# Pinning the input-gate product behind the recurrence's decay, with a tile of its own for the decay

## The chip, the core and the metric

The kernel runs on one core of one Trainium2 chip. The metric is the device time of one execution in microseconds (us); less is better. A core has five engines that matter here, each working through its own queue of instructions in order: PE (matrix products; PEld is its weight load), DVE (elementwise work and scans), ACT (functions and casts), POOL (small elementwise work and some DMA issues) and SP (DMA issues). An instruction starts when it is first in its queue and the semaphores that it waits for have been raised by other engines or by landed DMAs.

## The reference, cut to what matters

A trunk of two post-norm layers over 512 tokens of width 1024, in float32. The first layer (even) projects the input into eight retention heads and eight blocks of a gated linear recurrence (RG-LRU), multiplies both branches by SiLU gates, and maps them back; the second (odd) is differential attention. The change concerns the recurrence alone:

```
def rg_lru_branch(xb, conv_w, conv_b, wa, ba, wx, bx, lam):
    xc = causal_depthwise_conv(xb, conv_w) + conv_b
    xg = xc.reshape(B, S, LRU_BLOCKS, LRU_BLOCK_DIM)
    r = jax.nn.sigmoid(jnp.einsum('bsgi,gij->bsgj', xg, wa).reshape(B, S, W) + ba)
    i = jax.nn.sigmoid(jnp.einsum('bsgi,gij->bsgj', xg, wx).reshape(B, S, W) + bx)
    log_a = -LRU_C * r * jax.nn.softplus(-lam.astype(jnp.float32))
    a = jnp.exp(log_a)
    u = xc * i * jnp.sqrt(-jnp.expm1(2.0 * log_a))
    _, h = lax.associative_scan(combine, (a, u), axis=1)   # h = a * h_before + u
    return h
```

## The kernel before, in words

Activations lie with features on the 128 partitions and the 512 tokens along the row, so that a projection block is one 128x512 bank of PSUM. Every float32 operand of a product is split into a high part (a cast, L153, on ACT) and a low part (a subtraction, L154, on DVE), and each product is three matmuls (L158): high by high, low by high, high by low. A name that ends in h or l is such a part: k3h and k3l are the parts of head 3's key, w33h and w33l those of weight block 33.

The even layer runs over eight heads and eight recurrence blocks. Its projections are listed in one order: gl and gr (the gates), xb (the recurrence's input), q and k, out (a piece of the output projection). The smaller steps of retention and recurrence are generators that a helper (Side.tick) advances between the projection's matmuls. PE and SP run in the order in which the program is traced (manual_schedule). DVE, ACT and POOL are ordered by a scheduler, which works with priorities (the P_ numbers) and its own estimate of durations; the order is fixed when the kernel is built. keep_in_program_order pins an instruction behind the one that was traced last on its engine.

One recurrence block (lru) goes: L555 and L557 copy and scale the projection's bank xb_ps on ACT, which frees that bank; three L561 on DVE make the convolved block xc, which L153 and L154 split; PE makes the gates' products pr and pi; ACT takes the sigmoids (L570 to t, L575 to i) and a tanh (L577). L578 on DVE multiplies i by xc, the product that the change is about. Then d, made on DVE by L584 and L585 with two ACT results, the logarithm L582 and the exponential L583 in r, is the recurrence's decay; it is written over xc. L586 is a square root on ACT, L587 to L589 make the recurrence's factors, L590 is the scan, L593 applies the gate gl, and the result is split for the output projection (lrum). The tile i is the tile xb, so that L578 is the last reader of xc and L589 the first reader of the product.

Retention, beside it, makes scores rs by blocks (L515 on DVE multiplies by the decay mask dec, freeing one of two banks that pr and pi share), splits them (r20 is head 2, block 0), sums them with v into ro, squares (L526) and splits that into rq, and sums rq's square over the head by a product with ones (rv, L532 and L533). L537 to L548 normalize the head and apply gr.

Temporaries of both come from one pool of ten 128x512 tiles (es); the gate weights gw, which SP loads, take their place in it too. Projection banks are four and go round. Weights are loaded through three buffers w_r, each reused when the low part of the block three before has been made.

Of the kernel before, what the change touches and what calls it, by code (L numbers as in the profile page):

```python
# [11 lines left out]
ALU = mybir.AluOpType  # L12
# [92 lines left out]
def trunk(ctx: ExitStack, tc: tile.TileContext, a):  # L105
    nc = tc.nc
# [25 lines left out]
    def temp(name):  # L132
        return es.tile([P, S], F32, tag="es", name=name)

    def bank(pl, tag, name):
        return pl.tile([P, 512], F32, tag=tag, name=name)
# [4 lines left out]
    def part(n, name):  # L141
        return pair(sp, [P, n], f"s{n}", name, bufs=full if n == S else 1)

    def cut(t, *ix):
        return t[0][ix], t[1][ix]

    def split(src, dst, scale=None, copy=nc.scalar.copy):
        if scale is not None:
            s = sg[:, scale:scale + 1]
            nc.scalar.activation(out=dst[0], in_=src, func=AF.Identity, scale=s)  # L150
            nc.vector.scalar_tensor_tensor(out=dst[1], in0=src, scalar=s, in1=dst[0].bitcast(F32), op0=ALU.mult, op1=ALU.subtract)
            return
        copy(out=dst[0], in_=src)  # L153
        return nc.vector.tensor_tensor(out=dst[1], in0=src, in1=dst[0].bitcast(F32), op=ALU.subtract)  # L154

    def mm3(out, l, r, start, stop, kinds=range(3), **kw):
        for n in kinds:
            nc.tensor.matmul(out=out, lhsT=l[n == 2], rhs=r[n == 1], start=start and n == 0, stop=stop and n == 2, **kw)  # L158
# [392 lines left out]
    def lru(c, ps, m):  # L551

        with tc.high_priority(P_OUT if c in OUT_NEXT else P_CONV):
            xb = temp(f"xbp{c}")
            nc.scalar.copy(out=xb, in_=ps)  # L555
            xc = temp(f"xc{c}")
            nc.scalar.activation(out=xc, in_=ps, func=AF.Identity, scale=conv_w(3, c), bias=conv_b(c))  # L557
        with tc.high_priority(P_CONV):
            for w in range(3):
                sh = 3 - w  # L560
                nc.vector.scalar_tensor_tensor(out=xc[:, sh:], in0=xb[:, :S - sh], scalar=conv_w(w, c), in1=xc[:, sh:], op0=ALU.mult, op1=ALU.add)  # L561
        with tc.high_priority(P_OUT if c in OUT_NEXT or c == 7 else P_GATES):
            t2 = part(S, f"xc{c}")
            split(xc, t2)
        yield LRU_GATES[c]
        pr = bank(ps_sc, "sc", f"pr{c}")
        o = c % 2 * 2 * P
        mm3(pr, cut(gw[0], ALL, slice(o, o + P)), t2, True, True)
        t = temp(f"t{c}")
        nc.scalar.activation(out=t, in_=pr, func=AF.Sigmoid, bias=gba(c))  # L570
        yield 1
        pi = bank(ps_sc, "sc", f"pi{c}")
        mm3(pi, cut(gw[0], ALL, slice(o + P, o + 2 * P)), t2, True, True)
        i = xb
        nc.scalar.activation(out=i, in_=pi, func=AF.Sigmoid, bias=gbx(c))  # L575

        nc.scalar.activation(out=t, in_=t, func=AF.Tanh, scale=sp4[:, c:c + 1])  # L577
        nc.vector.tensor_tensor(out=i, in0=i, in1=xc, op=ALU.mult)  # L578
        d = xc
        r = temp(f"r{c}")  # L580

        nc.scalar.activation(out=r, in_=t, func=AF.Ln, bias=1.0)  # L582
        nc.scalar.activation(out=r, in_=r, func=AF.Exp, scale=-1.0)  # L583
        nc.vector.scalar_tensor_tensor(out=d, in0=t, scalar=1.0, in1=r, op0=ALU.add, op1=ALU.mult)  # L584
        nc.vector.scalar_tensor_tensor(out=d, in0=d, scalar=2.0, in1=r, op0=ALU.subtract, op1=ALU.mult)  # L585
        nc.scalar.activation(out=r, in_=t, func=AF.Sqrt)  # L586
        nc.vector.scalar_tensor_tensor(out=t, in0=t, scalar=1.0, in1=d, op0=ALU.subtract, op1=ALU.mult)  # L587
        nc.vector.scalar_tensor_tensor(out=r, in0=r, scalar=-2.0, in1=d, op0=ALU.mult, op1=ALU.mult)
        nc.vector.tensor_tensor(out=r, in0=r, in1=i, op=ALU.mult)  # L589
        nc.vector.tensor_tensor_scan(out=d, data0=t, data1=r, initial=0.0, op0=ALU.mult, op1=ALU.add)  # L590
        if ("gl", c) not in gates:
            yield lambda: 0 if ("gl", c) in gates else math.inf
        nc.vector.tensor_tensor(out=d, in0=d, in1=gates.pop(("gl", c)), op=ALU.mult)  # L593
        split(d, cut(m, ALL, c % 2))
# [18 lines left out]
    for kind, i in ev:  # L613
        if kind == "v":
            if i:
                for j in range(4):
                    side.need(job["ret", j], lambda: j in seen)
            v = v_even(i)
        elif kind == "xb":
            if i % 2 == 0:  # L620
                raw = load(f"gw{i}", [P, 4 * P], a["gw"][i // 2], pl=es, tag="es")
                gw[0] = pair(two, [P, 4 * P], "gw", f"gw{i}", bufs=1)
                split(raw, gw[0])
            job["lru", i] = side.add(lru(i, t_unit(x, f"xb{i}"), mixes(("lru", i // 2))), "lru", 2)
        elif kind == "q":
            dec[i] = load(f"dec{i}", [P, S], a["dec"][i], pl=two, tag="dec")
            q[i] = rope(t_unit(x, f"q{i}"), "q", f"q{i}")
        elif kind == "k":
            job["ret", i] = side.add(retention(i, q.pop(i), rope(t_unit(x, f"k{i}"), "k", f"k{i}"), v, dec.pop(i), mixes(("ret", i // 2))), "ret", 1, RET_START[i])
        elif kind in ("ro", "lo", "out"):  # L630
            even_out({"ro": ("ret",), "lo": ("lru",), "out": ("lru", "ret")}[kind], i, f"{kind}{i}")
        else:
            ps = t_unit(x, f"{kind}{i}")
            if len(users) >= 5:
                side.need(job[users[-5]])
            users.append(("ret" if kind == "gr" else "lru", i))
            g = gp.tile([P, S], F32, tag="g", name=f"{kind}{i}")
            with tc.high_priority(P_OUT if kind == "gl" and i in OUT_NEXT else 0):
                silu(ps, g, f"{kind}{i}")
            gates[kind, i] = g  # L640
# [425 lines left out]
```

## Time and profile before

| what | value |
|---|---|
| median of 3 runs | 919.75 us (917.55 to 919.83) |
| the profiled execution | 919.09 us, its span 917.3 us (1.8 us lie around the span) |
| PE busy | 904.7 us, 99% of the span |
| DVE busy | 717.7 us, 78% |
| ACT busy | 518.1 us, 56% |
| mean granted TensorE clock | 0.997 |

PE's busy time is an overlap: a 128x512 matmul is shown as 0.39 us long, and the next one starts 0.23 us after it. Whether PE stood still is read from the distance between starts, and not from the busy time.

### The profile page before, as it was taken

What the parts mean: (1) busy time and instruction counts of PE and PEld (TensorE: products, weight loads), DVE (VectorE), ACT (ScalarE), POOL (GpSimd) and SP (SyncE); (2) the same over time, 40 slices, a digit from 0 to 9 for tenths busy, and PEclk for the clock granted to TensorE, in tenths of its full rate; (3) what the DMA queues carried; (4) which work ended last, traced back from release to release, by engine and by line L of the source; (5) the groups of instructions that cost most, each with busy time, mean ns of one, the idle gap of its engine ahead of it and who ended that gap; (6) DMA issues with size and microseconds to landing.
All of it is one profiled execution on the core that took longest, in us unless ns stands there. A gap on an engine that the chain in (4) does not pass through costs nothing.

```text
span 917.3 us, 11876 instructions
## 1 busy us (share of the span) xinstructions
PE 904.7 (99%) x4258; PEld 750.2 (82%) x4258; DVE 717.7 (78%) x1191; ACT 518.1 (56%) x847; POOL 111.5 (12%) x190
## 2 busy tenths in 40 slices
PE   8999999999999999999999999999999999999996
PEld 6888887888888888888888878888887888888885
DVE  5877977978868998897778787748867668877687
ACT  5567796656575668532455666435755355665440
POOL 2311010120102010010101110000110100201112
PEclk9999999999999999999999999999999999999998
DMA  8985463682829372434942126547247282186102
GB/s 287 290 273 149 129 182 91 190 258 58 267 78 279 100 210 78 154 113 155 335 164 79 62 68 237 222 165 249 70 138 271 119 319 93 60 284 255 45 1 92
DMA packets 46524, 152.93 MB, mean 167 GB/s; under 512 B 6145, under 2 KB 6273, under 8 KB 45697
## 3 DMA queue, kind: packets, MB, share of 16 engines
q1 hardware_dynamic: 41472, 135.39, 41.8%
q0 software_dynamic: 4992, 16.78, 9.4%
q8 instruction: 33, 0.54, 0.2%
q14 instruction: 27, 0.21, 0.1%
HBM read 139.57 MB, written 37.75 MB: 193 GB/s over the span
## 4 chain that ended last, share of the span: by engine, by line
PE 87%; DVE 5%; ACT 3%; issue 2%; POOL 1%; DMA 1%; SPq 0%; DVEq 0%; ACTq 0%; POOLq 0%
PE oo_ps L158 8%; PE q_ps L158 5%; PE gr_ps L158 5%; PE gl_ps L158 4%; PE k_ps L158 4%; PE xb_ps L158 4%; PE ev_ps L158 4%; PE out_ps L158 4%; PE po L158 3%; PE as L158 3%; PE ov_ps L158 2%; PE gv3a L158 2%; PE eo_ps L158 2%; PE og_ps L158 2%; PE gv2a L158 2%; PE gv3b L158 2%
## 5 line engine op out<-in xcount | busy, mean ns | idle before, releaser
L701 ACT ACTIVATE e<-as,nm 128x128 f32<-128x128 f32 (+3 forms) x64 | 33.2, 523 | 33.2 <-DVE nm L698 33.0
L708 POOL TENSOR_SCALAR zr<-z 128x1 f32<-128x1 f32 x32 | 16.3, 510 | 248.7 <-ACT e L701 248.7
L740 DVE SCALAR_TENSOR_TENSOR o<-po,ars,og 128x256 f32<-128x256 f32 x32 | 15.5, 484 | 35.9 <-POOL ars L396 35.9
L187 POOL DMA_DIRECT2D t<-t x24 | 18.9, 788 | 160.9 <-DMA t<-in_od_w 160.9
L187 POOL DMA_DIRECT2D t<-in_od_w x24 | 19.0, 793 | 117.6 <-DMA t<-in_od_w 117.5
L737 POOL TENSOR_SCALAR ave<-ss,zr 128x1 f32<-128x1 f32 x32 | 15.8, 493 | 142.0 <-ACT po L734 133.7
L698 DVE CUSTOM_DVE_ANT_0 as<-as,mask 128x128 f32<-128x128 f32 (+3 forms) x64 | 30.4, 505 | 2.3 <-PE as L158 2.3
L734 ACT ACTIVATE po<-po 128x256 f32<-128x256 f32 x32 | 11.9, 371 | 25.6 <-PE po L158 25.3
L396 POOL TENSOR_TENSOR ars<-ave,nhalf 128x1 f32<-128x1 f32 x32 | 18.8, 586 | 2.7
L578 DVE TENSOR_TENSOR xbp<-xbp,xc 128x512 f32<-128x512 f32 x8 | 5.5, 691 | 17.0 <-ACT xbp L575 17.0
L709 DVE SCALAR_TENSOR_TENSOR e<-e,zr,e 128x128 f32<-128x128 f32 (+3 forms) x32 | 17.6, 549 | 0.8
L561 DVE SCALAR_TENSOR_TENSOR xc<-xbp,vecs,xc 128x509 f32<-128x509 f32 (+2 forms) x24 | 17.8, 744 | 0.2
L396 POOL TENSOR_TENSOR lrs<-lve,nhalf 128x1 f32<-128x1 f32 x8 | 7.3, 911 | 82.1 <-DVE lve L410 82.1
L279 DVE TENSOR_TENSOR y<-oo_ps,y 128x512 f32<-128x512 f32 x23 | 15.3, 684 | 2.2 <-PE oo_ps L158 2.2
L515 DVE TENSOR_TENSOR rsd<-rs,dec 128x512 f32<-128x512 f32 (+3 forms) x32 | 15.3, 482 | 0.7 <-PE rs L158 0.5
L570 ACT ACTIVATE t<-pr,vecs 128x512 f32<-128x512 f32 x8 | 5.5, 687 | 17.3 <-PE pr L158 17.3
L713 PE MATMUL wt<-ident,e 128*128 128x128 f32 x80 | 13.9, 272 | 0.0
L153 ACT CAST hh<-ht 128x512 fp32r<-128x512 f32 x8 | 4.7, 588 | 15.4 <-PE ht L658 15.4
L713 PEld LDWEIGHTS wt<-ident,e 128*128 128x128 f32 x80 | 10.5, 140 | 3.4
L586 ACT ACT_TABLE_LOAD x8 | 10.3, 1283 | 4.2 <-DVE xc L585 4.1
L701 ACT ACTIVATION_READ_ACCUMULATOR e<-as,nm 128x1 f32 x64 | 12.5, 195 | 0.0
L744 PEld LDWEIGHTS po<-ident,o 128*128 128x128 f32 x64 | 8.9, 140 | 4.2
(2844 smaller groups left out, 3472.6 us busy)
## 6 DMA issues: line engine op xcount, KB each, us to landing
w_r<-in_od_w SPq DMA_DIRECT2D x58, 512.0 KB, 5.9
w_r<-in_ev_w SPq DMA_DIRECT2D x47, 512.0 KB, 5.6
t<-in_od_w SPq DMA_DIRECT2D x48, 256.0 KB, 5.7
sx<-sd SPq DMA_DIRECT2D x24, 512.0 KB, 6.2
w_r<-t SPq DMA_DIRECT2D x24, 512.0 KB, 3.2
w_r<-in_ev_wo SPq DMA_DIRECT2D x16, 512.0 KB, 4.2
w_r<-in_od_wo SPq DMA_DIRECT2D x16, 512.0 KB, 4.8
t<-in_od_w POOLq DMA_DIRECT2D x24, 256.0 KB, 5.7
```

The lines of the kernel that those rows point to most:

```text
L158: nc.tensor.matmul(out=out, lhsT=l[n == 2], rhs=r[n == 1], start=start and n == 0, stop=stop and n == 2, **kw)
L187: nc.gpsimd.dma_start(out=dst, in_=two, max_dma_last_dim=4 * D, accum_op=ALU.add)
L279: nc.vector.tensor_tensor(out=yy, in0=ps, in1=yy, op=ALU.add)
L396: nc.gpsimd.tensor_tensor(out=out, in0=var, in1=nhalf[:, :1], op=ALU.pow)
L561: nc.vector.scalar_tensor_tensor(out=xc[:, sh:], in0=xb[:, :S - sh], scalar=conv_w(w, c), in1=xc[:, sh:], op0=ALU.mult, op1=ALU.add)
L698: nc.vector.tensor_tensor_reduce(out=ps[:, :n], in0=ps[:, :n], in1=mask[:, S - n:], scale=-QK_SCALE, scalar=3.0e38, op0=ALU.add, op1=ALU.m ...
L701: nc.scalar.activation(out=e, in_=ps[:, :n], func=AF.Exp, scale=-1.0, bias=nm, accum_out=z[:, mp:mp + 1])
L708: nc.gpsimd.tensor_scalar(out=zr[:, 1:2], in0=z[:, 0:1], scalar1=z[:, 0:1], scalar2=EPS, op0=ALU.mult, op1=ALU.mult)
L709: nc.vector.scalar_tensor_tensor(out=ee[0], in0=ee[1], scalar=zr[:, 0:1], in1=ee[0], op0=ALU.mult, op1=ALU.add)
L713: nc.tensor.transpose(out=pt[:, kb * P:kb * P + P], in_=ee[0][:, kb * P:kb * P + P], identity=ident)
L737: nc.gpsimd.tensor_scalar(out=ve, in0=ss, scalar1=zr[:, 1:2], scalar2=None, op0=ALU.add)
L740: nc.vector.scalar_tensor_tensor(out=o, in0=po[:, :2 * P], scalar=rs, in1=gates[qb, hd // 2][:, hc:hc + 2 * P], op0=ALU.mult, op1=ALU.mult)
```

## The change

The decay d gets a tile of its own from the pool of temporaries, so xc stays whole while d is made. The product of i and xc is traced behind the two operations that make d, and is pinned behind the second of them. One more tile per block is taken from the pool of ten; the number of operations on DVE, PE, POOL and SP stays the same. L578 becomes L585, and L582 to L585 become L581 to L584.

```diff
@@ lru @@
         nc.scalar.activation(out=t, in_=t, func=AF.Tanh, scale=sp4[:, c:c + 1])
-        nc.vector.tensor_tensor(out=i, in0=i, in1=xc, op=ALU.mult)
-        d = xc
+        d = temp(f"d{c}")
         r = temp(f"r{c}")
 
         nc.scalar.activation(out=r, in_=t, func=AF.Ln, bias=1.0)
         nc.scalar.activation(out=r, in_=r, func=AF.Exp, scale=-1.0)
         nc.vector.scalar_tensor_tensor(out=d, in0=t, scalar=1.0, in1=r, op0=ALU.add, op1=ALU.mult)
         nc.vector.scalar_tensor_tensor(out=d, in0=d, scalar=2.0, in1=r, op0=ALU.subtract, op1=ALU.mult)
+        tc.keep_in_program_order(nc.vector.tensor_tensor(out=i, in0=i, in1=xc, op=ALU.mult))
         nc.scalar.activation(out=r, in_=t, func=AF.Sqrt)
```

The scheduler answers with another order on DVE and ACT through the whole even layer; PE, SP and POOL keep theirs. Three places follow, each as it stands in the program before and then in the changed one.

On ACT, where block 3's bank is read (the projection that follows it is a piece of the output, out), before:

```order
L153 CAST lrum1h<-xc_1063 128x512
L555 COPY xbp_1379<-xb_ps 128x512
L557 ACTIVATE xc_1381<-xb_ps,vecs 128x512
L153 CAST retm0h<-rq_1168 128x512
L153 CAST r20h<-rsd_1328 128x512
L153 CAST r21h<-rsd_1370 128x384
```

and now:

```order
L153 CAST lrum1h<-d_1204 128x512
L153 CAST r20h<-rsd_1331 128x512
L153 CAST retm0h<-rq_1170 128x512
L555 COPY xbp_1382<-xb_ps 128x512
L557 ACTIVATE xc_1384<-xb_ps,vecs 128x512
L153 CAST r21h<-rsd_1373 128x384
```

The two reads of the bank, L555 and L557, moved behind two casts, one of a score block and one of retention's result.

On DVE, in block 4's turn, where head 3's squares are split (rq3l), before:

```order
L154 TENSOR_TENSOR w36l<-w_r,w36h 128x1024
L154 TENSOR_TENSOR rq3l<-rq_1950,rq3h 128x512
L154 TENSOR_TENSOR q4l<-q_c,q4h 128x512
L584 SCALAR_TENSOR_TENSOR xc_1825<-t_1909,r_1921 128x512
L585 SCALAR_TENSOR_TENSOR xc_1825<-xc_1825,r_1921 128x512
```

and now:

```order
L154 TENSOR_TENSOR w36l<-w_r,w36h 128x1024
L154 TENSOR_TENSOR q4l<-q_c,q4h 128x512
L583 SCALAR_TENSOR_TENSOR d_1924<-t_1913,r_1925 128x512
L584 SCALAR_TENSOR_TENSOR d_1924<-d_1924,r_1925 128x512
L154 TENSOR_TENSOR rq3l<-rq_1955,rq3h 128x512
L585 TENSOR_TENSOR xbp_1827<-xbp_1827,xc_1829 128x512
```

rq3l moved from in front of q4l and the two steps of d to behind them, and the product stands behind it.

On DVE, in block 6's turn, from the key's last step to the split of head 5's third score block (r52l), before:

```order
L384 TENSOR_TENSOR k_c<-k_c,k_s 128x512
L154 TENSOR_TENSOR r53l<-rsd_2850,r53h 128x128
L584 SCALAR_TENSOR_TENSOR xc_2695<-t_2774,r_2786 128x512
L154 TENSOR_TENSOR k6l<-k_c,k6h 128x512
L585 SCALAR_TENSOR_TENSOR xc_2695<-xc_2695,r_2786 128x512
L154 TENSOR_TENSOR r52l<-rsd_2806,r52h 128x256
```

and now:

```order
L384 TENSOR_TENSOR k_c<-k_c,k_s 128x512
L584 SCALAR_TENSOR_TENSOR d_2791<-d_2791,r_2792 128x512
L585 TENSOR_TENSOR xbp_2699<-xbp_2699,xc_2701 128x512
L154 TENSOR_TENSOR k6l<-k_c,k6h 128x512
L515 TENSOR_TENSOR rsd_2813<-rs_2809,dec_2556 128x256
L515 TENSOR_TENSOR rsd_2857<-rs_2853,dec_2556 128x128
L279 TENSOR_TENSOR y<-lo_ps_2848,y 128x512
L154 TENSOR_TENSOR r53l<-rsd_2857,r53h 128x128
L587 SCALAR_TENSOR_TENSOR t_2780<-t_2780,d_2791 128x512
L588 SCALAR_TENSOR_TENSOR r_2792<-r_2792,d_2791 128x512
L154 TENSOR_TENSOR r52l<-rsd_2813,r52h 128x256
```

The product and the mask step of that block came from in front of the key's first step to behind its last one, and one y step (L279) and two steps of the recurrence (L587, L588) now stand ahead of r52l.

## Rows read from the trace of the kernel before

**Rows 1.** The page's first part, PE's row: busy us, share of the span and instructions, for PE and the other engines.

```profile
PE 904.7 (99%) x4258; PEld 750.2 (82%) x4258; DVE 717.7 (78%) x1191; ACT 518.1 (56%) x847; POOL 111.5 (12%) x190
```

**Rows 2.** The view of busy time by stretches, the even layer from 48 to 412 us: length, then busy us (and instructions) of PE, PEld, DVE, ACT and POOL, then the granted clock, the DMA engines' share and GB/s.

```profile
48.00:412.00 364.00, 363.11 (x1656) 300.74 (x1656) 304.78 (x462) 234.79 (x309) 35.93 (x45) 1.00 0.56 162
```

**Rows 3.** The timeline of PE at eight places of the even layer: start us, duration us, engine, line, operation, out<-in, shape.

```profile
113.51 0.39 PE L158 MATMUL q_ps<-xh,w17l 128*128 128x512 f32 x1
113.73 0.39 PE L158 MATMUL pr<-xc2h,gw2h 128*128 128x512 f32 x1
114.12 0.50 PE L158 MATMUL pr<-xc2l,gw2h 128*128 128x512 f32 x1
...
139.33 0.39 PE L158 MATMUL out_ps<-w21h,lrum0l 128*128 128x512 f32 x1
140.23 0.39 PE L158 MATMUL rs<-q2h,k2h 128*128 128x256 f32 x1 [0.52 <-DVE rsd L515]
...
141.39 0.39 PE L158 MATMUL out_ps<-w21h,lrum0h 128*128 128x512 f32 x1
...
147.92 0.39 PE L158 MATMUL pr<-xc3h,gw2h 128*128 128x512 f32 x1
148.69 0.50 PE L158 MATMUL pr<-xc3l,gw2h 128*128 128x512 f32 x1 [0.38 <-DVE xc3l L154]
149.02 0.40 PE L158 MATMUL pr<-xc3h,gw2l 128*128 128x512 f32 x1
...
189.59 0.40 PE L158 MATMUL rs<-q3h,k3l 128*128 128x512 f32 x1
...
212.47 0.39 PE L533 MATMUL rv<-rq3l,ones 128*128 128x512 f32 x1
...
316.68 0.28 PE L158 MATMUL ro<-r52l,ev12h 128*128 128x256 f32 x1
...
362.15 0.22 PE L158 MATMUL rs<-q7h,k7h 128*128 128x128 f32 x1
```

**Rows 4.** The timeline of DVE around 134 to 141 us, block 2's and block 3's turn (columns as in rows 3; in brackets the idle time before and what ended it).

```profile
134.91 0.69 DVE L485 TENSOR_TENSOR gl<-gl_ps,gl_sg 128x512 f32<-128x512 f32 x1
...
139.49 1.15 DVE L515 TENSOR_TENSOR rsd<-rs,dec 128x512 f32<-128x512 f32 x2
```

**Rows 5.** The timeline of ACT from 139 to 141 us.

```profile
139.01 0.62 ACT L153 CAST lrum1h<-xc 128x512 fp32r<-128x512 f32 x1 [2.25 <-DVE xc L593]
139.53 0.58 ACT L555 COPY xbp<-xb_ps 128x512 f32<-128x512 f32 x1
140.01 0.78 ACT L557 ACTIVATE xc<-xb_ps,vecs 128x512 f32<-128x512 f32 x1
```

**Rows 6.** The view of the tile w_r, the one load that SP issues between 180.9 and 181.3 us, that of weight block 33: the issue, and its us to landing.

```profile
L179 SPq DMA_DIRECT2D w_r<-in_ev_w x1: 328/328/328, 181.0 to 181.0; - x1
...
DMA to landing us min/median/max: 6.1/6.1/6.1
```

**Rows 7.** The timelines of DVE and ACT around 188 us, where head 3's key and weight block 33 are split.

```profile
188.45 0.69 DVE L154 TENSOR_TENSOR k3l<-k_c,k3h 128x512 fp32r<-128x512 f32 x1 [0.69 <-ACT k3h L153]
189.40 1.23 DVE L154 TENSOR_TENSOR w33l<-w_r,w33h 128x1024 fp32r<-128x1024 f32 x1 [0.26 <-ACT w33h L153]
...
187.80 0.62 ACT L153 CAST k3h<-k_c 128x512 fp32r<-128x512 f32 x1 [3.29 <-DVE k_c L384]
```

**Rows 8.** The timelines of DVE and ACT from 207 to 214 us, block 4's turn.

```profile
211.61 0.69 DVE L154 TENSOR_TENSOR rq3l<-rq,rq3h 128x512 fp32r<-128x512 f32 x1 [1.27 <-ACT rq3h L153]
...
212.82 0.68 DVE L584 SCALAR_TENSOR_TENSOR xc<-t,r 128x512 f32<-128x512 f32 x1
213.54 0.69 DVE L585 SCALAR_TENSOR_TENSOR xc<-xc,r 128x512 f32<-128x512 f32 x1
...
207.59 1.03 ACT L153 CAST w36h<-w_r 128x1024 fp32r<-128x1024 f32 x1
...
209.14 1.28 ACT L583 ACT_TABLE_LOAD   x1
210.43 0.63 ACT L583 ACTIVATE r<-r 128x512 f32<-128x512 f32 x1
```

**Rows 9.** The timeline of DVE from 307 to 317 us, block 6's turn.

```profile
307.43 0.68 DVE L578 TENSOR_TENSOR xbp<-xbp,xc 128x512 f32<-128x512 f32 x1
308.03 0.41 DVE L515 TENSOR_TENSOR rsd<-rs,dec 128x256 f32<-128x256 f32 x1
309.71 0.69 DVE L378 TENSOR_TENSOR k_c<-k_ps,cos 128x512 f32<-128x512 f32 x1 [1.26 <-PE k_ps L158]
...
314.66 0.42 DVE L154 TENSOR_TENSOR r52l<-rsd,r52h 128x256 fp32r<-128x256 f32 x1
```

**Rows 10.** The timeline of DVE from 360 to 363 us, block 7's turn; the first of the two steps in the upper row is the mask of head 7's second score block.

```profile
360.71 0.88 DVE L515 TENSOR_TENSOR rsd<-rs,dec 128x384 f32<-128x384 f32 x2
361.51 1.21 DVE L154 TENSOR_TENSOR w59l<-w_r,w59h 128x1024 fp32r<-128x1024 f32 x1
```

**Rows 11.** The view of line 578, the product before: how long DVE sat idle in front of it in all (us, times), and until what.

```profile
  ACT xbp L575: 17.0, 7
```

**Rows 12.** The timelines of SP at 70 us (the load of gate weights 2) and of ACT at 100 us (the first use of weight block 17, which SP issues behind it).

```profile
70.59 0.34 SPq L162 DMA_DIRECT2D gw<-in_gw  x1
...
100.16 1.04 ACT L153 CAST w17h<-w_r 128x1024 fp32r<-128x1024 f32 x1
```

## The prediction

> **What bounds the kernel now.** I read the page's first part, then busy time by stretches, then PE's timeline for the distances between starts. PE is shown busy 99% of the span [rows 1], and 363.11 of 364 us of the even layer, at a granted clock of 1.00 [rows 2]. Busy time alone would hide a stall, but the starts confirm it: a 512-column matmul starts 0.22 to 0.23 us after the one before (113.51 to 113.73), and where this step is longer PE waited [rows 3]. In the even layer I find three such places over 0.1 us. At 114.12 the step is 0.39 instead of 0.23, at 140.23 it is 0.90, at 148.69 it is 0.77. Behind a stall the next 512-column step is 0.33 (148.69 to 149.02) instead of 0.23, so a stall costs 0.10 more than its wait. The three are worth 0.26, 0.77 and 0.64 us, 1.67 in all. The rest of the layer is matmuls at their pace, and their number and order stay.
>
> So the change cannot shorten PE's work. It can win at most these 1.67 us, and it loses wherever the new order of DVE and ACT delivers an operand, or frees a bank, later than PE asks for it. The sum is therefore a list of places: for each matmul that waits for DVE or ACT in the changed program, how early its operand was, and what now stands ahead of it.
>
> **The change part by part.** The operations are the same, but for one table load less on ACT (51 to 50, in block 7's turn). The product was waited in front of by 17.0 us of idle DVE, seven times, for the sigmoid L575 [rows 11]; moved, it leaves that idle time and takes its 0.60 us where DVE is busy. Nothing off the even layer's recurrence moves.
>
> Units. Independent 512-wide DVE steps start 0.60 us apart (rq3l at 211.61, two steps later L584 at 212.82), dependent ones 0.72 (212.82 to 213.54), and each lasts 0.68 to 0.69 [rows 8]. A 1024-wide one, 1.21 to 1.23 long [rows 7, 10], takes 1.14 by the same overlap, a 256-wide one 0.33, its 0.41 less the same 0.08 [rows 9]. Casts on ACT start 0.52 apart, the copy to L557 0.48 [rows 5]. From an end to the start that waits: 0.03 to an elementwise engine (k3h ends 188.42, k3l starts 188.45 [rows 7]), 0.06 to PE (the first rsd ends at 139.49 + 0.68 = 140.17, PE starts 140.23 [rows 3, 4]).
>
> 1. Out's fourth bank (PE 141.39). It is the xb bank, freed by L557, which ended at 140.01 + 0.78 = 140.79, so 0.60 early [rows 3, 5]. Now two casts stand in front of it. r20h needs the mask step rsd, whose start I leave at 139.49: between gl, which starts when its sigmoid is there (134.91), and rsd, one 512-wide step left (L548) and another came (L541) [rows 4]. So r20h starts at 140.20. retm0h needs L548, now the step behind rsd, from 140.09 to 140.77: retm0h at 140.80, L555 at 141.32, L557 from 141.80 to 142.58, PE at 142.64. That is 1.25 + 0.10 = **+1.35**. The stall at 140.23 stays.
>
> 2. Block 3's gate product (148.69). PE now asks for xc3l 1.35 later. xc3l itself comes little later: the three convolution steps wait for L557, but the queue ahead of them had filled the time, and w25l (1.14) fell behind it. The 0.64 goes: **-0.64**.
>
> 3. Block 2's gate product (114.12). The gate step gr (0.60) and a small split fell behind xc2l. PE waited 0.16: **-0.26**.
>
> 4. Head 3's key (189.59). w33h and w33l now stand ahead of k3h and k3l. The load of block 33 lands 181.0 + 6.1 = 187.13 [rows 6], and ACT was idle until 187.80 [rows 7], so w33h runs 187.16 to 188.21 and k3h is little later. w33l starts at 188.25, k3l 1.14 later at 189.39, to 190.08: PE at 190.14 instead of 189.59, 0.55 + 0.10 = **+0.65**.
>
> 5. Head 3's squares (212.47). On ACT w36h ends at 208.62; then table load (1.28), exponential, and only then the casts: q4h at 210.45, the square 210.97, rq3h 211.58 to 212.18, which is in time. On DVE q4l starts at 211.11, d's two steps at 211.71 and 212.43, rq3l at 213.03 to 213.72. PE at 213.78 instead of 212.47: 1.31 + 0.10 = **+1.41** [rows 3, 8].
>
> 6. Head 5's third score block (316.68). The product and a 256-wide mask step ran before the key's first step, which waits for PE with 1.26 us idle [rows 9]. They now come behind it, and one y step and L587, L588 stand ahead of r52l too: 4 x 0.60 + 0.33 = 2.73. r52l starts at 314.66 + 2.73 = 317.39, ends 317.81, PE at 317.87 instead of 316.68: 1.19 + 0.10 = **+1.29**.
>
> 7. Head 7's last score block (362.15). It wants the bank that the first rsd of 360.71 frees, at about 361.26. w59l (1.14) now stands ahead: 362.40, PE 362.46, 0.31 + 0.10, **+0.40** [rows 3, 10].
>
> Sum: 1.35 - 0.64 - 0.26 + 0.65 + 1.41 + 1.29 + 0.40 = +4.20 us. Against the profiled execution, 919.09 us (917.3 of span), this makes 923.3 us; the median of the runs shown is 0.66 above that execution, which I do not add.
>
> Bounds. Item 1: at least 0.7 if rsd comes 0.60 earlier, because L548 no longer precedes it; no gain in item 2 at worst. Item 4: nothing if the load lands 0.6 sooner, 1.2 if as much later. Items 5 and 6: 1.0 to 1.6 each, by one step more or less. Item 7: 0 to 0.8. Item 3: nothing won at worst. From both sides: +1.8 and +7.2, so 920.9 to 926.3. I take the walk's own value, since each step of it is a row.
>
> SP keeps its order, but the load of gate weights 2, at 70.59, now finds its place in the pool only when a score tile freed about 3 us later is done, and weight block 17 is issued behind it. That costs nothing: block 17 is first cast at 100.16 [rows 12], some 20 us after it lands. Without that cover it would cost the 3 us.
>
> **A rule weighed against the rows.** The rows show independent DVE steps 0.60 apart at 0.68 of duration [rows 8]. The Trainium skill, VectorE: DVE Perf Modes, section "The DRAIN you can't avoid", says that the next operation does not start until the pipe has emptied; by that rule each step that is moved ahead would cost its whole duration, 0.08 more, about 0.8 over the ten steps of items 1 to 7, and the sum would be 5.0. The trace disagrees, since its starts overlap.
>
> **The rivals.**
> - Cover absorbs it. Each stall makes PE later, and a chain not tied to PE (item 4's load) has that much more time; items 4 and 7 vanish, 5 and 6 are a step shorter: +4.20 - 1.05 - 1.2 = +2.0, 921.1 us. For it: the slacks are a few tenths and one step decides. Against it: the chains of items 1, 5 and 6 start from PE's own banks and move with it. 0.20.
> - Not slower, by a head start. Where the product stood in front of a rope, DVE waited for the sigmoid with the rope queued behind it [rows 11]; without it the rope starts up to 0.60 earlier. If what follows is early by that much, items 1 and 4 to 7 are met, and the won places remain: 919.09 - 1.67 = 917.4 us. The point that decides is item 5: rq3l would have to end by 212.41, 1.31 before my walk; the head start is 0.60 and the exponential on ACT, not the rope, is last there. 0.06.
> - The pin orders the product but frees nothing, and one step more or less per block on DVE (8 x 0.60 at most, at 78% busy [rows 1]) never reaches PE: 919.1 us. Against it stand the reordered casts of item 1. 0.04.
> - Each step costs its whole duration: 919.09 + 5.0 = 924.1 us. This is the mechanism of the rule above; the starts in rows 8 speak against it. 0.03.
> - The pool's extra tile holds SP: 3 us more on the forecast's sum, 926.3 us. Against it the cover of 20 us. 0.02.
>
> **How the numbers follow.** The forecast has 0.65 and its own range 921.3 to 925.0 us. A difference under 0.3% (2.76 us here) can't be told from no change. Of the forecast some 0.06 lies under +2.76, which with most of the cover rival (0.17), the head start's gain of under 0.3% (0.04) and the third rival (0.04) makes 0.31 for no change. Slower has the rest of the forecast, 0.59, of the cover rival 0.03, and the last two, 0.05: 0.67. Faster keeps 0.02, of the head start. The range of 8 in 10 reaches down to 920.0, into the cover rival, and up to 925.2.
>
> **What would show it.** In the changed profile PE's steps should be long at the places of items 1, 4, 5, 6 and 7, by 1.25, 0.55, 1.31, 1.19 and 0.31, with L557, k3l, rq3l, r52l and the rsd as what it waited for, and even where blocks 2's and 3's gate products start; the odd layer should last as long as before. I am wrong if these steps are even (the head start), if they are long and the span has not grown, or if SP's loads come last before a matmul.

## The result, and the profile after

The changed kernel takes 922.93 us, the median of 6 runs (921.58 to 924.58), beside 918.90 us of the kernel before in 6 runs (917.55 to 919.83). The ratio is 1.0049, with a 95% interval of 1.0039 to 1.0059: slower by 4.0 us. The forecast was 923.3 us. The profiled execution takes 923.08 us, its span 921.3 us, against 919.09 and 917.3 before; the granted clock is 0.998.

First the busy time by stretches, as in [rows 2]: the first line is the even layer, the second the odd one, and the first two numbers are the length of the stretch and PE's busy time in it.

```profile
48.00:416.00 368.00, 363.69 (x1653) 300.10 (x1653) 305.27 (x462) 233.81 (x308) 35.90 (x45) 1.00 0.55 161
416.00:921.00 505.00, 495.93 (x2416) 413.34 (x2414) 380.28 (x680) 258.12 (x503) 62.53 (x111) 1.00 0.44 158
```

In the even layer PE was busy 363.11 of 364 us before [rows 2]; now it is busy 363.69 of 368. Nearly the same work (1656 and 1653 matmuls) has 4.31 us of idle time in it instead of 0.89. The odd layer is as it was: from its first product to the end of the span, 511.1 us (410.18 to 921.3) beside 511.2 (406.12 to 917.3, its row is below). So PE's timeline of the even layer is the view to read next: start, duration, instruction, and in brackets the idle time in front of it and what ended it.

```profile
28.23 0.47 PE L158 MATMUL gl_ps<-xh,w4h 128*128 128x512 f32 x1
...
113.28 0.39 PE L158 MATMUL pr<-xc2h,gw2h 128*128 128x512 f32 x1
113.51 0.39 PE L158 MATMUL pr<-xc2l,gw2h 128*128 128x512 f32 x1
...
139.51 0.39 PE L158 MATMUL rs<-q2h,k2h 128*128 128x256 f32 x1 [0.52 <-DVE rsd L515]
...
140.43 0.40 PE L158 MATMUL out_ps<-w22h,lrum0l 128*128 128x512 f32 x1
141.93 0.50 PE L158 MATMUL out_ps<-w21h,lrum0h 128*128 128x512 f32 x1 [1.10 <-ACT xc L557]
142.27 0.40 PE L158 MATMUL out_ps<-w21l,lrum0h 128*128 128x512 f32 x1
...
148.56 0.39 PE L158 MATMUL pr<-xc3h,gw2h 128*128 128x512 f32 x1
148.78 0.39 PE L158 MATMUL pr<-xc3l,gw2h 128*128 128x512 f32 x1
...
189.42 0.40 PE L158 MATMUL rs<-q3l,k3h 128*128 128x512 f32 x1
190.44 0.50 PE L158 MATMUL rs<-q3h,k3l 128*128 128x512 f32 x1 [0.62 <-DVE k3l L154]
...
213.24 0.50 PE L532 MATMUL rv<-rq3h,ones 128*128 128x512 f32 x1
214.74 0.50 PE L533 MATMUL rv<-rq3l,ones 128*128 128x512 f32 x1 [1.01 <-DVE rq3l L154]
...
319.02 0.28 PE L158 MATMUL ro<-r52h,ev12h 128*128 128x256 f32 x1
320.31 0.39 PE L158 MATMUL ro<-r52l,ev12h 128*128 128x256 f32 x1 [1.01 <-DVE r52l L154]
...
365.68 0.39 PE L158 MATMUL gr_ps<-xh,w56l 128*128 128x512 f32 x1
366.12 0.33 PE L158 MATMUL rs<-q7h,k7h 128*128 128x128 f32 x1
...
410.18 0.48 PE L158 MATMUL ov_ps<-w64h,hh 128*128 128x512 f32 x1
```

A step is the time from one start to the next, and its pitch is what it lasts where PE waits for nothing. Behind a 512-column matmul the pitch is 0.23 (113.28 to 113.51, 148.56 to 148.78), behind a 256-column one 0.12; from 213.24 to 214.74 the step is 1.50. I call a step even where it is within 0.05 of its pitch. Over the pitch that gives, with the row in the kernel before that it answers to [rows 3]:

| item, place | step over its pitch before | after | with the 0.10 to 0.11 behind a stall |
|---|---|---|---|
| 1, out's fourth bank | none | 1.27 | +1.38 |
| 2, block 3's gate product | 0.54 | none | -0.64 |
| 3, block 2's gate product | 0.16 | none | -0.26 |
| 4, head 3's key | none | 0.79 | +0.90 |
| 5, head 3's squares | none | 1.28 | +1.39 |
| 6, head 5's third score block | none | 1.17 | +1.28 |
| 7, head 7's last score block | none | 0.21 | +0.31 |
| score step of head 2 (140.23 before) | 0.68 | 0.68 | 0 |

The sum is +4.36. To compare kernels I use one stretch of PE's timeline: from the first product of a gate in the even layer (28.23) to the odd layer's first product (410.18), here 381.95 us. In the kernel before these two rows are

```profile
28.68 0.47 PE L158 MATMUL gl_ps<-xh,w4h 128*128 128x512 f32 x1
...
406.12 0.48 PE L158 MATMUL ov_ps<-w64h,hh 128*128 128x512 f32 x1
```

or 377.44 us. The stretch is 4.51 longer, of which the table's places make 4.36. The other 0.15 lies in two small steps that were even before: 0.08 at the key's product with q3l (189.42) and 0.07 at block 6's gate product (307.68). In front of the stretch this execution took 0.45 less (28.23 against 28.68).

ACT and DVE show the queues behind the long steps. On ACT, ahead of item 1 and of item 4:

```profile
139.49 0.62 ACT L153 CAST r20h<-rsd 128x512 fp32r<-128x512 f32 x1 [0.43 <-DVE rsd L515]
140.09 0.62 ACT L153 CAST retm0h<-rq 128x512 fp32r<-128x512 f32 x1
140.62 0.58 ACT L555 COPY xbp<-xb_ps 128x512 f32<-128x512 f32 x1
141.10 0.78 ACT L557 ACTIVATE xc<-xb_ps,vecs 128x512 f32<-128x512 f32 x1
...
187.47 1.06 ACT L153 CAST w33h<-w_r 128x1024 fp32r<-128x1024 f32 x1 [4.43 <-DMA w_r<-in_ev_w]
```

The two casts stand in front of the copy and of L557, which ends at 141.88; PE starts at 141.93. On DVE, item 4, item 5, and the last steps of items 6 and 7:

```profile
188.56 1.23 DVE L154 TENSOR_TENSOR w33l<-w_r,w33h 128x1024 fp32r<-128x1024 f32 x1 [0.93 <-ACT w33h L153]
189.70 0.69 DVE L154 TENSOR_TENSOR k3l<-k_c,k3h 128x512 fp32r<-128x512 f32 x1
...
212.06 0.69 DVE L154 TENSOR_TENSOR q4l<-q_c,q4h 128x512 fp32r<-128x512 f32 x1 [1.23 <-ACT q4h L153]
212.67 0.69 DVE L583 SCALAR_TENSOR_TENSOR d<-t,r 128x512 f32<-128x512 f32 x1
213.39 0.69 DVE L584 SCALAR_TENSOR_TENSOR d<-d,r 128x512 f32<-128x512 f32 x1
214.00 0.68 DVE L154 TENSOR_TENSOR rq3l<-rq,rq3h 128x512 fp32r<-128x512 f32 x1
...
319.84 0.41 DVE L154 TENSOR_TENSOR r52l<-rsd,r52h 128x256 fp32r<-128x256 f32 x1
...
357.94 0.68 DVE L515 TENSOR_TENSOR rsd<-rs,dec 128x512 f32<-128x512 f32 x1
...
365.51 0.55 DVE L515 TENSOR_TENSOR rsd<-rs,dec 128x384 f32<-128x384 f32 x1
```

The squares' low half rq3l stood at 211.61 in front of the query's and of the decay's two steps [rows 8]; now it stands behind all three. The product itself has no idle time in front of it any more, where it had 17.0 us [rows 11], and no place that PE waits for came earlier by it; in the view by lines (busy in all and mean ns of one, then idle time before them):

```profile
L585 DVE TENSOR_TENSOR xbp<-xbp,xc 128x512 f32<-128x512 f32 x8 | 5.5, 684 | 0.0
```

### The profile page after: what moved, and what is told of

Read it like the earlier page. It is cut to its first block, busy times and chain, and to the rows that moved or that the text cites. A ratio compares the mean times of both kernels' runs of the same rounds, so it can differ in the third digit from the quotient of the medians.

```text
span 921.3 us, 11868 instructions
## 1 busy us (share of the span) xinstructions
PE 906.0 (98%) x4258; PEld 750.3 (81%) x4258; DVE 718.5 (78%) x1191; ACT 517.3 (56%) x846; POOL 111.8 (12%) x190
## 4 chain that ended last, share of the span: by engine, by line
PE 78%; DVE 9%; ACT 6%; DMA 3%; issue 2%; POOL 1%; SPq 0%; DVEq 0%; ACTq 0%; POOLq 0%
PE oo_ps L158 8%; PE q_ps L158 4%; PE xb_ps L158 4%; PE ev_ps L158 4%; PE k_ps L158 3%; PE out_ps L158 3%; PE gr_ps L158 3%; PE gl_ps L158 3%; PE po L158 3%; PE as L158 3%; PE ov_ps L158 2%; PE gv3a L158 2%; PE eo_ps L158 2%; PE og_ps L158 2%; DMA w_r<-in_ev_w 2%
## 5 line engine op out<-in xcount | busy, mean ns | idle before, releaser
L279 DVE TENSOR_TENSOR y<-oo_ps,y 128x512 f32<-128x512 f32 x23 | 15.3, 684 | 2.2 <-PE oo_ps L158 2.2
L378 DVE TENSOR_TENSOR q_c<-q_ps,cos 128x512 f32<-128x512 f32 x8 | 5.5, 686 | 11.4 <-PE q_ps L158 11.4
L706 DVE RECIPROCAL zr<-z 128x1 f32<-128x1 f32 x32 | 5.2, 162 | 9.3 <-ACT e L701 9.1
```

Of the source, the lines that this page charges most:

```text
L279: nc.vector.tensor_tensor(out=yy, in0=ps, in1=yy, op=ALU.add)
```

## The experiments

The theory (A in the expectations): each long step comes from the order in which the build put DVE's and ACT's steps, and the time is the sum of these places. The rivals: the pin or the product's new place costs a share per block; a place is late for another reason than the steps ahead of it; what is mended at one place comes back at the next. Times are medians beside the kernel before in the same series (918.7, 918.52 and 918.2 us in the three series). The stretch is read from the two PE rows named above; what it is longer than before's 377.44 is the sharper measure, since the time in front of it varied by up to 1.8 us between the traces (27.73 to 29.57); the last section comes back to that.

**The tile alone.**

```
-        d = xc
+        d = temp(f"d{c}")
```

The product stays at its old line, not pinned.

> The decay has its own tile, the product stands at its old place and is not pinned. Theory A (the loss is made at the places where the build orders DVE and ACT otherwise, and the tile alone already moves three of them): PE's steps are long at the squares rq3l by 1.28, at the score block r52l by 1.17 and at the last rsd by 0.21, and even at block 2's gate product, while 140.2 and 148.7 stay long as before and nothing is long at out's fourth bank and at the key k3l; 1.39 + 1.28 + 0.21 - 0.26 = +2.62, 921.5 us. Theory B (the pin makes the loss, the tile is free): 918.9 us and before's three stalls. Theory C (each of the eight moved products costs an equal share, 4.0 / 8 = 0.5 us, on DVE): no product is moved, 918.9 us.

Measured: 921.08 us, ratio 1.0025 (1.0016 to 1.0035). The stretch is 380.58, +3.14. PE's timeline:

```profile
213.13 0.50 PE L533 MATMUL rv<-rq3l,ones 128*128 128x512 f32 x1 [1.01 <-DVE rq3l L154]
...
318.90 0.39 PE L158 MATMUL ro<-r52l,ev12h 128*128 128x256 f32 x1 [1.17 <-DVE r52l L154]
```

Items 5 (1.28) and 6 (1.43) are there without a pin, and out's bank is in time. The last rsd was even, which theory A had missed by 0.2, and the key was 0.16 over its pitch, which it had not foreseen. The tile by itself makes more than half of the loss; theories B and C fall.

**The whole change in some blocks only.**

```
+        own = c in (4, 6, 7)
+        if not own:
+            nc.vector.tensor_tensor(out=i, in0=i, in1=xc, op=ALU.mult)
+        d = temp(f"d{c}") if own else xc
...
+        if own:
+            tc.keep_in_program_order(nc.vector.tensor_tensor(out=i, in0=i, in1=xc, op=ALU.mult))
```

> The whole change, tile and pin, in recurrence blocks 4, 6 and 7 alone; the other five are as before. Theory A: the squares rq3l, the score block r52l and the last rsd are late as in the changed kernel, 1.39 + 1.28 + 0.21 = +2.88, 921.8 us; before's stalls at 114.1, 140.2 and 148.7 stay. Theory C (an equal share per block): 3 x 0.5 = +1.5, 920.4 us.

Measured: 922.51 us, ratio 1.0037 (1.0023 to 1.0050), stretch 380.74, +3.30. PE is long at the squares by 1.28, at r52l by 1.44, at the last rsd by 0.23, and before's three stalls are there. The complement, with `c not in (4, 6, 7)`:

> The whole change in blocks 0, 1, 2, 3 and 5 alone; blocks 4, 6 and 7 are as before. Theory A: out's fourth bank and the key k3l are late, 1.38 + 0.90, and block 2's and 3's gate products are even, -0.26 - 0.64: +1.38, 920.3 us; no long step at rq3l, r52l and the last rsd. Theory C: 5 x 0.5 = +2.5, 921.4 us. Together with the kernel that changes blocks 4, 6 and 7, theory A wants the two differences to add up to the changed kernel's 4.0 to 4.3.

Measured: 920.46 us, ratio 1.0014 (1.0004 to 1.0025), stretch 378.44, +1.00; long are out's bank (1.27) and the key (0.50), and blocks 2's and 3's gate products are even. The key was expected at 0.79. The two stretches add up to 4.30, against 4.51 for the whole change, and three blocks make three quarters of it: no equal share per block. The medians do not add up so well, 3.8 and 1.8 against 4.0; in the traces of these two kernels the time in front of the stretch was 0.9 and 0.5 longer than before.

**The same tiles and the same pin in blocks 4, 6 and 7, but another tile is the extra one.** The hyperbolic tangent writes the extra tile, and the decay goes into the tile that the sigmoid left.

```
+        own = c in (4, 6, 7)
+        s = t
+        if own:
+            t = temp(f"d{c}")
+        nc.scalar.activation(out=t, in_=s, func=AF.Tanh, scale=sp4[:, c:c + 1])
...
+        d = s if own else xc
```

> As the kernel with the change in blocks 4, 6 and 7, with as many tiles and the same pin, but the extra tile is first written by the hyperbolic tangent and the decay goes into the tile that the sigmoid left. Theory A in its sharper form (the pool hands its tiles out in program order at their first write, so whatever is named behind the decay's tile is queued behind the decay's first step): the squares, the score block and the last rsd are in time again, 918.9 us with before's three stalls. Rival (the extra tile or the pinned product itself costs the 2.9): 921.8 us, as with the late tile. Theory C: 920.4 us.

Measured: 919.30 us, ratio 1.0008 (0.9999 to 1.0017), stretch 377.57, +0.13. ACT's timeline in block 4, first with the late tile:

```profile
209.54 1.28 ACT L585 ACT_TABLE_LOAD   x1
210.83 0.63 ACT L585 ACTIVATE r<-r 128x512 f32<-128x512 f32 x1
...
211.88 0.59 ACT L526 ACTIVATE rq<-ro 128x512 f32<-128x512 f32 x1
212.50 0.62 ACT L153 CAST rq3h<-rq 128x512 fp32r<-128x512 f32 x1
```

and with the early one:

```profile
209.34 0.59 ACT L526 ACTIVATE rq<-ro 128x512 f32<-128x512 f32 x1
...
210.34 0.62 ACT L153 CAST rq3h<-rq 128x512 fp32r<-128x512 f32 x1
210.97 1.28 ACT L588 ACT_TABLE_LOAD   x1
```

The square of head 3 (L526) now runs ahead of the exponential (the table load of L588 belongs to it), as in the kernel before, and all three places are even. So neither the number of tiles nor the pin costs anything by itself in these blocks. The two kernels differ in the step that first writes the extra tile, and with it in how long the sigmoid's tile is held; their times do not tell these two apart. The first fits a pool whose tiles the build hands out in program order, each at its first write: rq3, rsd52 and the group norm's tile of head 6 are named behind d4, d6 and d7, and the decay's first step is written only after the exponential, while the tangent comes early. That the build works so is concluded from the orders of these two kernels and from their times; no run shows the pool itself.

**One order of the changed kernel set back by hand.** `queue` puts steps behind a first one on the same engine when the program is built, without a wait on the chip; `mark` keeps each step under the name of what it writes (`xc3` is L557 of block 3, `retm1` the split of head 1's output). It moves the line numbers by 10. For item 1:

```
+    def queue(first, *later):
+        for x in later:
+            tc.add_manual_dep(mark[x], mark[first].name, mybir.DependencyInfo(mybir.DependencyClass.NoSync, mybir.DependencyReason.DATA), reason="queue")
...
+    queue("xc3", ("r20", "h"), ("retm1", "h"))
```

> The changed kernel, with one order set by hand: on ACT the two casts r20h and retm0h stand behind the convolution's start L557 of block 3, as before. Theory A (item 1: the bank is freed late because of these two casts): the long step at 141.9 (1.27 + 0.11) goes, all the others stay; what block 3's gate product then does is open: if its low half xc3l is tied to L557, it comes earlier too and stays in time, -1.38, 921.5 us; if it is tied to the queue of DVE, up to 0.64 comes back, 922.2 us. Rival (the bank is late for another reason, the score step rsd at 140): the step stays, 922.9 us.

Measured: 921.40 us, ratio to the kernel before 1.0036 (1.0024 to 1.0049), stretch 380.70, 1.25 less than the changed kernel. The long step at out's bank is gone, and block 3's product is late again, by 0.47 (with 0.11 behind it), as

```profile
148.17 0.50 PE L168 MATMUL pr<-xc3l,gw2h 128*128 128x512 f32 x1 [0.31 <-DVE xc3l L164]
```

shows. The casts were the cause. Block 3's product is tied to DVE's queue, and w25l stands behind xc3l here as in the changed kernel: there it was PE's delay at out's bank that made the product even, so items 1 and 2 are one pair. The key was less late in this trace, 0.32, since the cast w33h, which waits for block 33's load, started 1.0 earlier (186.45 against 187.47) while PE asked for the key only 0.55 earlier; with the key as late as in the changed kernel the gain would have been 1.38 - 0.58 = 0.80, near the second case of the expectation (922.2 us).

For item 4:

```
+    queue(("k3", "h"), ("w33", "h"))
+    queue(("k3", "l"), ("w33", "l"))
```

> The changed kernel, with one order set by hand: the two steps of weight block 33 stand behind those of head 3's key on ACT and DVE. Theory A (item 4): the long step at 190.4 (0.79 + 0.11) goes, all the others stay, 922.9 - 0.90 = 922.0 us. Rival (the key is late by its own chain, as rope and cast came later): the step stays, 922.9 us.

Measured: 921.31 us, ratio 1.0031 (1.0020 to 1.0043), stretch 381.03, 0.92 less than the changed kernel. The step to k3l is 0.24; every other place is as in the changed kernel. Here the sum of places was right to 0.02.

**The kernel before, with the order of block 4 alone.** Neither tile nor pin:

```
+    queue("exp4", "square3")
+    queue(("q4", "h"), "square3")
+    queue(("q4", "l"), ("rq3", "l"))
+    queue("e4", ("rq3", "l"))
```

(`e4` is the decay's second step of block 4.)

> The kernel before, with neither tile nor pin; only the order of block 4 is set by hand to that of the changed kernel: on ACT the exponential and the query's cast ahead of the square of head 3, on DVE the query's low half and the decay's two steps ahead of rq3l. Theory A (the order alone makes item 5): PE's step at the squares is long by 1.28 + 0.11, before's three stalls stay, 918.8 + 1.39 = 920.2 us. Rival (it takes the tile, its wait for a place in the pool or its traffic, to be late): 918.8 us, step even.

Measured: 919.63 us, ratio 1.0015 (1.0006 to 1.0024), stretch 378.83, +1.39.

```profile
211.73 0.50 PE L542 MATMUL rv<-rq3h,ones 128*128 128x512 f32 x1
213.24 0.50 PE L543 MATMUL rv<-rq3l,ones 128*128 128x512 f32 x1 [1.00 <-DVE rq3l L164]
```

The step is 1.51, beside 1.50 in the changed kernel, and apart from the step behind it no other step of the stretch moved by more than 0.06. The order alone makes item 5.

**Mending what is left.** The change in blocks 0, 1, 2, 3 and 5, the two orders set by hand for items 1 and 4, and one more, meant to shorten the stall at 140 (`rsd20` is head 2's first score step, `gn1` the scale step L544 of head 1's group norm):

```
+    queue("rsd20", "gn1")
```

> The change in blocks 0, 1, 2, 3 and 5 alone, with the orders of the two kernels that set one by hand, and the first score step rsd of head 2 ahead of the group norm's scale step L544 on DVE. Theory A: no long step is left of items 1, 4, 5, 6, 7, blocks 2's and 3's gate products stay even (-0.26, -0.64), and the stall at 140 falls from 0.68 to about 0.1 (-0.6): 918.8 - 1.5 = 917.3 us, 918.0 if block 3's product is late again. Rival (a step won at one place is lost at the next, so that the sum of the places is not the time): 918.8 us or more.

Measured: 920.86 us, ratio 1.0024 (1.0015 to 1.0034), stretch 378.63, +1.19 where -1.5 was expected. The stall at 140 fell to 0.22, and another came. DVE and PE:

```profile
144.32 0.74 DVE L571 SCALAR_TENSOR_TENSOR xc<-xbp,vecs,xc 128x510 f32<-128x510 f32 x1
144.98 1.22 DVE L164 TENSOR_TENSOR w24l<-w_r,w24h 128x1024 fp32r<-128x1024 f32 x1
```

```profile
143.68 0.45 PE L168 MATMUL out_ps<-w24h,retm0h 128*128 128x512 f32 x1
146.25 0.50 PE L168 MATMUL out_ps<-w24l,retm0h 128*128 128x512 f32 x1 [2.12 <-DVE w24l L164]
```

The build, given these orders, put weight block 24's low half behind two convolution steps and the split r21l. It started 1.78 later than with the same five blocks and no order set (144.98 against 143.20), while PE, no longer held at out's bank, asked for it 1.7 earlier; PE's step was 2.35 over its pitch. The places still add up to the stretch: 0.22 and 0.10 at 140, 0.11 behind out's bank, 2.35 and 0.11 at w24l make 2.89, less before's 1.68, or +1.21. What failed is the assumption that an order set at one place stays local. Without the last order, and with xc3l ahead of the residual's first step (`queue(("xc3", "l"), "out000", ("w25", "l"))`):

> The change in blocks 0, 1, 2, 3 and 5 alone; the two casts behind the convolution's start of block 3, the steps of weight block 33 behind the key's, and on DVE xc3l ahead of the residual's first step L277. The score step of head 2, which pushed w24l back by 3 us in the kernel before this one, is left at its place. Theory A: the stall at 140 stays (0.68), out's fourth bank, the key, rq3l, r52l, the last rsd and block 2's product are even, w24l is in time, and block 3's product waits 0.1 to 0.2 instead of 0.54; from the first gate product of the even layer to the odd layer's first product 377.4 - 0.26 - 0.4 = 376.8 us, the time 918.5 - 0.65 = 917.9 us. Rival (each order that is set by hand moves a loss to another place): 377.4 us or more for that stretch, 918.5 us or more.

Measured: 918.01 us beside 918.20, ratio 0.9995 (0.9986 to 1.0004), stretch 376.96, 0.48 less than before. All of the change's long steps are gone, w24l is in time, and block 3's product is 0.18 over its pitch. The stretch is as expected to 0.2; the time can't be told from the kernel before.

**Item 2 by itself**, on the kernel before:

```
+    queue(("xc3", "l"), ("w25", "l"))
```

> The kernel before with one order set by hand: weight block 25's low half behind xc3l on DVE. Theory A (item 2: w25l, 1.14 on DVE, is what made block 3's product late): a residual step of 0.60 takes its place ahead of xc3l, which comes 0.54 earlier; PE's step at block 3's product falls from 0.54 over its pitch to under 0.1, the other two stalls stay, the stretch from the first gate product to the odd layer's first product is 377.4 - 0.6 = 376.8 us and the time 917.9 us. Rival (xc3l waits for its high half on ACT, so its place in the queue of DVE is free): the step stays 0.54, 377.4 us, 918.5 us.

Measured: 917.45 us beside 918.20, ratio 0.9997 (0.9988 to 1.0006), stretch 376.91, 0.53 less than before.

```profile
147.23 0.39 PE L168 MATMUL pr<-xc3h,gw2h 128*128 128x512 f32 x1
147.51 0.50 PE L168 MATMUL pr<-xc3l,gw2h 128*128 128x512 f32 x1
```

The step to xc3l is 0.28 instead of 0.77. It was w25l's place in the queue that made block 3's product late in the kernel before. The one order without the change gives as much as the mended change. Neither of the last two kernels is faster by more than a measurement of the time can tell.

## Why the prediction was right, and where not

The forecast of 923.3 us met 922.93, and the profiled execution's +3.99 a sum of +4.20; of these 3.99 the even layer's stretch has +4.51, and the time in front of it -0.45. So the places were right, but that the total came within 0.21 is partly luck: the stretch is 0.31 over the sum, and the shorter time in front of it, for which the prediction has no term, took that back. Its steps:

- Where the time would go. PE's work stayed, the odd layer stayed, and the five long steps and two even ones are at the seven places named, with the operands named as what ended each wait. The stall at 140 stayed.
- Item 1: 1.35 forecast, 1.38 measured; the casts are the cause, as setting them back showed. Item 2: -0.64 and -0.64; that w25l made the stall is shown on the kernel before. Of the two reasons given for its end, PE's delay is the one that carries it: with w25l behind xc3l, but out's bank in time, the product was late by 0.47. Item 3: -0.26 and -0.26; no run took it alone.
- Item 4: 0.65 forecast, 0.90 measured. The mechanism holds (setting the order back took 0.92 away), but the term for the load was too small: w33h, which waited for its load, started at 187.47, not at 187.16. In three kernels with the same order here the step was 0.79, 0.50 and 0.32. It hangs on a landing that varies, and it was the one term of the sum that was tied to a load and not to PE's own steps.
- Items 5 and 6: 1.41 and 1.29 forecast, 1.39 and 1.28 measured. Counting steps in the queue at 0.60 and 0.72 each was enough. For item 5 the order alone gave +1.39 in the kernel before. Item 6 was not taken alone: the runs show its queue, and that it goes together with items 5 and 7 when the extra tile is written early.
- Item 7: 0.40 forecast, 0.31 measured. Its reason was wrong, though its size was near, which is luck. The mask step ended 0.89 ahead of PE before (361.26 to 362.15 [rows 3, 10]) and ends 0.15 behind the time at which PE would have started now (366.06, against 366.12 - 0.21), so it came 1.04 later, near the 1.14 of w59l. But w59l stands far ahead of it (356.80), in front of the mask step of head 7's first score block, and that step came 0.69 earlier beside PE. What made the second one late stands between the two: 7.57 us (357.94 to 365.51) where there were 5.84 (354.87 to 360.71), with three more steps of the group norm (L540, L541, L543).
- The two misses are +0.25 and -0.09; with them the seven places make 4.36, and the two small steps, which the prediction did not have, the other 0.15. The upper bound was added wrongly: its terms make +6.55, or 925.6 us, and not +7.2. Items 4 to 7 as measured lie inside the bounds given for them.
- The rivals. Cover did not make any place shorter than the walk by more than the 0.09 of item 7. The head start, if there was one (the product's idle time went from 17.0 to 0.0 us), reached no place that PE waits for. The pin did change orders. SP's load of gate weights 2 was issued at 73.84 instead of 70.59, and nothing waited for it. In the rival by which each step costs its whole duration, the trace after speaks against it as the one before did: q4l starts at 212.06 and the next step at 212.67, 0.61 apart at 0.69 of duration. The prediction took half of what the Trainium skill says in VectorE: DVE Perf Modes, section "The DRAIN you can't avoid": the same paragraph adds that a next operation that is not held starts earlier. The trace disagrees with the first half alone and agrees with that addition.

What the prediction did not say is which half of the change does it. It spoke of the pin's order throughout, and the extra tile was looked at only for SP. The runs give the tile by itself +3.14 of the stretch, by way of the order, and items 5 and 6 are its work, as is the end of item 3's stall; items 1 and 2 and most of item 4 come only with the product's new, pinned place. No run has the new place without the pin.

## What to carry to other kernels

Where one engine is busy 99% of a stretch, a change on the others is priced by walking, for each operand that the full engine waits for, the queue that now stands ahead of it; here seven such walks gave the stretch to within 0.31 us, one of them (item 7) by luck. A new tile in a shared pool is not free because it is small: here it changed the build's order on DVE and ACT, and giving the extra tile to an earlier writer took 3.2 of 3.3 us of the stretch back. An order set by hand at one place can push a step elsewhere (w24l, 2.35 us), so the whole stretch is read again after each.

## What the runs showed that was not expected

At the start PE's first products came at half their pace in some of the traces. In the kernel before, and in the one with the change in blocks 4, 6 and 7:

```profile
5.20 1.19 PE L158 MATMUL ev_ps<-w0h,xh 128*128 128x512 f32 x4 [0.72 <-ACT xh L356]
```

```profile
5.34 2.07 PE L158 MATMUL ev_ps<-w0h,xh 128*128 128x512 f32 x4 [0.52 <-ACT xh L356]
```

Four products last 1.19 in one and 2.07 in the other, with starts 0.43 apart instead of 0.23, for up to 4.4 us. The row from 5.40 to 7.40 in the latter shows 5 matmuls of PE, where the kernel before has 10, at the same granted clock of 1.00:

```profile
5.40:7.40 2.00, 2.00 (x5) 1.61 (x6) 1.60 (x3) 1.43 (x3) 0.00 (x0) 1.00 0.92 309
```

It was so in four of the twelve traces, and in these the stretch behind it began at 29.16 to 29.57, in the others at 27.73 to 28.68. These four are the kernels with the change in blocks 4, 6 and 7 (late tile and early tile), in the other five, and the first of the mended ones. In all four the medians differ from the kernel before by 0.5 to 1.2 more than the stretches do (3.81 against 3.30, 1.76 against 1.00, 0.60 against 0.13, 2.34 against 1.19); in the others by between 0.8 less and 0.3 more. So the slow start seems to belong to the kernel and not to the one execution that was traced. Its cause was not looked for and stays open. It is one reason why PE's stretch told these kernels apart more sharply than their times.
